# An eighth Strassen pair, a modulation row formed early and in place, and a down product that begins with two blocks kept in SBUF

## The chip, the cores and the metric

The kernel runs on one core of one Trainium2 chip. The time is device microseconds (us) of one execution of the whole layer, batch 1, 512 tokens, width 1024. It is given as the median of several runs; one more execution was recorded instruction by instruction, and every row below comes from that one.

## The reference

The layer is a hybrid mixer (an mLSTM and an S5 state space model, gated and mixed) followed by a convolutional gated FFN, each behind an adaptive layer norm. The change lies in the FFN and in what feeds it. Cut to that:

```python
def _conv_glu_ffn(h, w_ffn_up, w_ffn_conv, b_ffn_conv, w_ffn_down):
    val, gate = jnp.split(h @ w_ffn_up, 2, axis=-1)          # 1024 -> 2 x 2816
    gate = jax.nn.gelu(_causal_dwconv(gate, w_ffn_conv, b_ffn_conv))   # 3 taps along the tokens
    return (gate * val) @ w_ffn_down                          # 2816 -> 1024

mod = silu(c) @ w_ada + b_ada
sh1, sc1, g1, sh2, sc2, g2 = jnp.split(mod, 6, axis=-1)
...
h = _standardize(x) * (1.0 + sc2) + sh2
f = _conv_glu_ffn(h, w_ffn_up, w_ffn_conv, b_ffn_conv, w_ffn_down)
x = _layer_norm(ALPHA * x + (1.0 + g2) * f, ln2_gain, ln2_bias)
```

`g2` is one row of 1024 numbers, a product of the conditioning vector with 1024 x 1024 weights. The kernel multiplies it into the rows of `w_ffn_down` instead of into `f`.

## The kernel before

Products are in fp32 precision built from pairs: each operand is split into a high and a low part (a cast on ScalarE, line 226 or 1227, then a subtraction on VectorE, line 215), and one product of 128 x 128 weights with 128 x 512 activations is three matmuls (lines 247 to 249).

The FFN has 22 hidden blocks of 128 (`NF`), each with a gate product and a value product over 8 chunks of the width: 24 matmuls of 512 columns each. From block 0 on, the loop over `j` forms the blocks. A block whose number is in `FAST` is done together with its follower by `fast_and_plain`: block `j` by Strassen's scheme (its gate and value rows and the two token halves are the 2 x 2 matrix; seven products of 12 matmuls with 256 columns, line 1264), block `j + 1` in the plain way. Such a pair is called pair 6, pair 8 and so on after its first block; each Strassen product needs a combination of weights (`fast_operands`, VectorE line 212, tiles `hx`) split into halves (`half`, tiles `hb`), and combinations of activations that `x_combos` forms once, ahead of block `XJ` = 3.

PSUM tiles: the gate product of block `j` lies in `gtile[j % 2]` (two tiles called `acc`), the value product in `vtile[j % 2]` (two called `s`), and four tiles called `hd` serve the first two Strassen products, the gelu's scratch and whatever else asks. `gate_half` reads a gate tile by ScalarE once (line 1204) and by VectorE twice (line 207, 128x510 and 128x511, the two convolution taps), then forms the gelu (a Square and a Tanh on ScalarE, lines 567 and 569, each followed by one VectorE line 207). `val_half` multiplies by the value and either writes the block to DRAM (`spill`, blocks below `NSP` = 20) or keeps it split in SBUF (tiles `gab`).

`ada2_step` adds one eighth of `g2`'s product into two `s5h` tiles (`acc2[3]`): two loads from `wa` and two VectorE instructions (line 207). `MODS` lists after which blocks a step is done. At block `G2J` = 20, `grow` sums those tiles over the partitions with four matmuls against ones (line 951; they need the tiles split first, VectorE line 215) and forms the row in two `hh` tiles. At block `FJ` = 21, the first block of down weights is multiplied by `g2` and split (`scaled`: VectorE line 212, ScalarE and VectorE for the split).

Then `tail_product` runs the down product over the 22 blocks in the order of the list `down`: 14 places are streamed, each 24 matmuls onto eight PSUM tiles; the last eight are resident and go token block by token block, with the final layer norm behind each. `act_at` reads the spilled blocks back two places ahead. Tiles have tags with a fixed number of buffers (`BUFS`): `w`=2, `wh`=3, `wl`=3 for weights, `hb`=6, `hh`=7, `hx`=17, `s5h`=8.

Each engine takes its instructions in the fixed order that a scheduler wrote into the program when it was built, and all DMAs of the kernel are issued by one queue (SP) in its order. The scheduler follows the order of the code only loosely: it may place an instruction earlier or later on an engine, by its own estimate of when things are ready.

Of the kernel before, what the change touches and what calls it, by code (L numbers as in the profile page):

```python
# [16 lines left out]
P = 128  # L17
# [15 lines left out]
NF = 22  # L33
# [103 lines left out]
M2 = 2  # L137
MKR = 6
PF = 1
G2J = 20  # L140
FAST = (6, 8, 10, 12, 14, 16, 18)
XJ = 3
MODS = (5, 6, 8, 10, 12, 14, 16, 18)
NSP = 20
FJ = 21
QUICK = (1, 3)
LAST = ((0, 0, 512), (1, 0, 256), (1, 256, 512))
# [15 lines left out]
def _build(ctx, tc, nc, h):  # L163
# [14 lines left out]
    def bank(tag):  # L178
        return tl(tag, [P, 512], pool=ps)
# [10 lines left out]
    def hh(n=512, dt=F32, parts=P):  # L190
        return hx(n, dt, parts, "hh")
# [4 lines left out]
    def dma(o, i):  # L196
        return nc.sync.dma_start(o, i)  # L197

    def ts(o, i, a, b=None, op0=ALU.mult, op1=None):
        if op1 is None:  # L200
            V.tensor_scalar(o, i, a, None, op0=op0)
        else:
            V.tensor_scalar(o, i, a, b, op0=op0, op1=op1)

    def stt(o, i0, s, i1, op0=ALU.mult, op1=ALU.add, acc=None):
        if acc is None:
            V.scalar_tensor_tensor(o, i0, s, i1, op0=op0, op1=op1)  # L207
        else:
            V.scalar_tensor_tensor(o, i0, s, i1, op0=op0, op1=op1, accum_out=acc)
# [31 lines left out]
    def pair_of(x, tag):  # L241
        p = new_pair(tag)
        split_into(p[0], p[1], x)
        return p
# [698 lines left out]
        dma(r, h["rows"][i:i + 1, :].to_broadcast([P, D]))  # L943
        return [r[:, :512], r[:, 512:]]

    def grow(i, factor, tag="s5"):
        g = row(i)
        for n in range(2):
            o = bank(tag)
            for e, x in enumerate(pair_of(acc2[2 + i][n], "hh")):  # L950
                T.matmul(o, lhsT=onesr, rhs=x, start=e == 0, stop=e == 1)
            stt(g[n], o, 1.0, g[n], ALU.add, ALU.add)
            ts(g[n], g[n], factor)
        return g

# [256 lines left out]
    def val_half(j, gg, ov):  # L1212
        if len(ov) == 1:
            tt(gg, ov[0], gg)
        else:
            for i in range(2):
                sl = slice(256 * i, 256 * i + 256)
                tt(gg[:, sl], ov[i][:, 0:256], gg[:, sl])
        if j < NSP:
            dma(spill[j * P:(j + 1) * P, :], gg)  # L1220
            gp_.append(None)
        else:
            gp_.append(pair_of(gg, "gab"))

    def half(src):
        o = big((P, 2, 512), F32R, next(optag))
# [96 lines left out]
    first = []  # L1323
    for j in range(NF):
        if j == G2J:
            g2 = grow(1, 0.5, "hd")
        if j >= FJ:
            first.append(scaled(h["wfd"][len(first)], g2, None))
        if j == XJ:
            x_combos()  # L1330
        if j in FAST:
            fast_and_plain(j)
        elif j - 1 not in FAST:
            ou = {}
            for u in (2 * j + 1, 2 * j):
                if u in pre:
                    ou[u] = pre[u]
                else:
                    w = wsplit(h["wup"][u])
                    ou[u] = (gtile if u % 2 else vtile)[j % 2]  # L1340
                    up_mm(ou[u], w, slice(0, 512))
                if u % 2:
                    gg = gate_half(j, (ou[u],))
            val_half(j, gg, (ou[2 * j],))
        ada2_step(MODS.count(j))
    l2 = []

    def finish2(t, bk):
# [5 lines left out]
        for n in range(2):  # L1354
            dma(h["out"][t * P:(t + 1) * P, n * 512:(n + 1) * 512], r[n])
        yield
    down = list(range(NF))
    got = {}

    def act_at(k):  # L1360
        for kk in range(k, min(k + 3, NF)):
            j = down[kk]
            if kk in got:
                continue
            if j >= NSP:
                got[kk] = gp_[j]
                continue
            x = hh()
            dma(x, spill[j * P:(j + 1) * P, :])
            got[kk] = pair_of(x, "hx" if j % 7 < 3 else "s5h")  # L1370
        return got[k]

    tail_product(act_at, [h["wfd"][j] for j in down], g2, "hh", NF, 8, [("s5b", "s5b")] * 2 + [("hp", "hp")] * 4 + [("hb", "hb")] * 2, finish2, FDB, first)
# [17 lines left out]
```

## Time and profile before

| | |
|---|---|
| Median of 3 runs | 862.05 us (861.99 to 862.38) |
| The profiled execution | 859.15 us, of it 857.4 us from first to last instruction |
| TensorE (PE) busy | 818.5 us, 95% |
| VectorE (DVE) busy | 651.4 us, 76% |
| ScalarE (ACT) busy | 382.5 us, 45% |
| Mean granted TensorE clock | 0.997 of full speed |

The profiled execution lies 2.90 us below the median of the runs. In the profile, 527.23 us is the first matmul of block 4, 549.49 us the first of pair 6, 697.43 us the first of block 20, and 726.30 us the first of the down product. A row of a timeline gives start and duration in microseconds, engine, line, operation, the tile written and the tiles read (buffer numbers left out), the shape, and in square brackets the idle time of the engine before it with what ended that idle time.

### The profile page before, as it was taken

The page shows a single profiled execution, that of the slowest core. Times are in us where ns is not written, and L with a number is a line of the kernel's source. Part 1 is how long each engine was busy: PE and PEld are TensorE (multiplying, and loading weights), DVE is VectorE, ACT ScalarE, POOL GpSimd, SP SyncE. Part 2 cuts the span into 40 slices and gives each one's busy share as a digit, 9 for nine tenths or more (in the row PEclk, how much of TensorE's full clock was granted, in tenths as well). Part 3 has the DMA queues.
Part 4 walks back from the last instruction along what each step waited for, and adds up shares of the span by engine and source line. Part 5 has one row for each costly group of instructions (what it writes and reads, how often), then busy time and mean ns, then how long its engine had stood idle before and what let it go on. Part 6 is the DMA issues. An engine that isn't in the chain of part 4 may idle for free.

```text
span 857.4 us, 12051 instructions
## 1 busy us (share of the span) xinstructions
PE 818.5 (95%) x4358; PEld 672.8 (78%) x4358; DVE 651.4 (76%) x1260; ACT 382.5 (45%) x638; POOL 95.5 (11%) x233
## 2 busy tenths in 40 slices
PE   3999999999999999999999999999999997999996
PEld 1777868788687788888887988899888885888885
DVE  6557978789689774568978899878887667899144
ACT  4454564555546433232334565355555434545000
POOL 2871221122112100000002100000000000000000
PEclk9999999999999999999999999999999999999998
DMA  9922132222212233568655026544442233777011
GB/s 340 323 96 88 57 98 62 62 73 71 75 55 86 87 123 123 196 230 284 212 180 174 2 91 238 187 148 148 148 149 99 99 98 117 240 218 234 27 50 49
DMA packets 51179, 116.48 MB, mean 136 GB/s; under 512 B 14000, under 2 KB 14896, under 8 KB 51120
## 3 DMA queue, kind: packets, MB, share of 16 engines
q1 hardware_dynamic: 51120, 115.71, 40.9%
q8 instruction: 34, 0.56, 0.3%
q14 instruction: 25, 0.20, 0.1%
HBM read 106.25 MB, written 7.34 MB: 132 GB/s over the span
## 4 chain that ended last, share of the span: by engine, by line
PE 74%; DVE 13%; DMA 4%; ACT 4%; issue 2%; SPq 2%; POOL 0%; DVEq 0%; ACTq 0%; POOLq 0%
PE acc L247 10%; PE acc L249 10%; PE acc L248 10%; PE hd L247 6%; PE hd L248 6%; PE hd L249 6%; PE s L247 4%; PE s L249 4%; PE s L248 4%; PE acc L1264 3%; PE hd L1264 3%; DVE hh L207 3%; SPq L197 2%; DVE s5h L212 1%; DVE wl L215 1%
## 5 line engine op out<-in xcount | busy, mean ns | idle before, releaser
L226 ACT CAST wh<-w 128x1024 fp32r<-128x1024 f32 (+2 forms) x89 | 88.7, 999 | 126.8 <-PE acc L248 89.1
L215 DVE TENSOR_TENSOR wl<-w,wh 128x1024 fp32r<-128x1024 f32 (+2 forms) x89 | 103.4, 1165 | 34.5 <-ACT wh L226 33.7
L247 PE MATMUL acc<-hp,wh 128*128 128x512 f32 x256 | 103.0, 403 | 0.4 <-ACT hx L790 0.4
L249 PE MATMUL acc<-hp,wl 128*128 128x512 f32 x256 | 101.9, 398 | 0.0
L248 PE MATMUL acc<-hp,wh 128*128 128x512 f32 x256 | 101.7, 397 | 0.0
L1029 POOL TENSOR_SCALAR mov<-mov 128x1 f32<-128x1 f32 x6 | 3.6, 607 | 503.0 <-ACT acc L1028 330.8
L247 PEld LDWEIGHTS acc<-hp,wh 128*128 128x128 f32 x256 | 48.0, 188 | 14.2 <-issue 3.3
L249 PEld LDWEIGHTS acc<-hp,wl 128*128 128x128 f32 x256 | 48.1, 188 | 11.1 <-issue 0.4
L248 PEld LDWEIGHTS acc<-hp,wh 128*128 128x128 f32 x256 | 48.1, 188 | 10.7 <-issue 0.4
L207 DVE SCALAR_TENSOR_TENSOR s5h<-hh,k,s5h 128x512 f32<-128x512 f32 x56 | 39.7, 746 | 8.3 <-DMA hh<-in_wa 8.2
L207 DVE SCALAR_TENSOR_TENSOR hh<-hd,hh 128x512 f32<-128x512 f32 (+3 forms) x40 | 24.2, 607 | 15.7 <-POOL hh L859 8.4
L247 PE MATMUL hd<-s5b,wh 128*128 128x512 f32 (+1 forms) x88 | 31.9, 368 | 0.7 <-ACT s5b L1180 0.5
L248 PE MATMUL hd<-s5b,wh 128*128 128x512 f32 (+1 forms) x88 | 32.1, 366 | 0.2 <-DVE s5b L215 0.2
L249 PE MATMUL hd<-s5b,wl 128*128 128x512 f32 (+1 forms) x88 | 32.1, 366 | 0.0
L248 PE MATMUL acc<-hx,wh 128*128 128x512 f32 x77 | 30.4, 395 | 0.0
L247 PE MATMUL acc<-hx,wh 128*128 128x512 f32 x77 | 30.3, 394 | 0.0
L249 PE MATMUL acc<-hx,wl 128*128 128x512 f32 x77 | 30.3, 393 | 0.0
L1227 ACT CAST hb<-hx 128x512 fp32r<-128x512 f32 x28 | 17.4, 621 | 26.0 <-PE acc L1264 15.4
L226 ACT CAST hb<-hh 128x512 fp32r<-128x512 f32 (+3 forms) x37 | 20.3, 550 | 17.2 <-DVE hh L207 11.1
L212 DVE TENSOR_TENSOR hh<-w,hh 128x512 f32<-128x512 f32 x42 | 27.3, 684 | 0.5 <-DMA w<-in_wfd 0.3
L215 DVE TENSOR_TENSOR hb<-hh,hb 128x512 fp32r<-128x512 f32 (+3 forms) x37 | 22.1, 599 | 1.6 <-ACT hb L226 1.3
L1264 PEld LDWEIGHTS acc<-hp,hb 128*128 128x128 f32 x168 | 22.0, 188 | 1.3
(596 smaller groups left out, 2276.1 us busy)
## 6 DMA issues: line engine op xcount, KB each, us to landing
hh<-in_wa SPq DMA_DIRECT2D x64, 256.0 KB, 4.4
w<-in_win SPq DMA_DIRECT2D x30, 512.0 KB, 3.3
w<-in_wup SPq DMA_DIRECT2D x30, 512.0 KB, 3.4
w<-in_wfd SPq DMA_DIRECT2D x22, 512.0 KB, 4.1
hb<-in_wa SPq DMA_DIRECT2D x16, 512.0 KB, 7.3
gab<-in_wup SPq DMA_DIRECT2D x14, 512.0 KB, 4.0
spill<-hh SPq DMA_DIRECT2D x20, 256.0 KB, 2.3
hh<-spill SPq DMA_DIRECT2D x20, 256.0 KB, 3.4
```

The source lines that it names most:

```text
L197: return nc.sync.dma_start(o, i)
L207: V.scalar_tensor_tensor(o, i0, s, i1, op0=op0, op1=op1)
L212: V.tensor_tensor(o, a, b, op=op)
L215: V.tensor_tensor(o, a, b, op=ALU.subtract)
L226: A.copy(hi, x)
L247: T.matmul(o, lhsT=wh, rhs=xh, start=first, stop=False)
L248: T.matmul(o, lhsT=wh, rhs=xl, start=False, stop=False)
L249: T.matmul(o, lhsT=wl, rhs=xh, start=False, stop=last)
L1029: GP.tensor_scalar(v[:, 2:3], v[:, 0:1], v[:, 1:2], EPS * D, op0=ALU.add, op1=ALU.add)
L1227: A.copy(o[:, 0], src)
L1264: T.matmul(o[:, 0:256], lhsT=w[:, p, sl], rhs=x[k][y], start=first and k + i == 0, stop=k == 3 and i == 2, skip_group_check=True)
```

## The change

Pair 4 (blocks 4 and 5) is also done by Strassen's scheme. The eight steps of `g2` move forward (two after block 6, two after block 10, the last after block 14 instead of 18), and `g2` is formed ahead of pair 16 instead of block 20, in the two `s5h` tiles that held its sum, which it then occupies to the end; the bias row comes in through two passing `hh` tiles. Blocks 18 and 19 are not written to DRAM but kept split in two `hb` tiles, and the down product takes them first; the two last places, 20 and 21, stay as they were. The weights scaled at block 21 are then those of block 18. Spilled blocks are read back into `hx` and `s5h` tiles in turns of three and three instead of three and four.

```diff
-G2J = 20
-FAST = (6, 8, 10, 12, 14, 16, 18)
+G2J = 16
+FAST = (4, 6, 8, 10, 12, 14, 16, 18)
 XJ = 3
-MODS = (5, 6, 8, 10, 12, 14, 16, 18)
-NSP = 20
+MODS = (4, 6, 6, 8, 10, 10, 12, 14)
+NSP = 18
 FJ = 21
...
+    def grow_in_place(i, factor, tag):
+        g = acc2[2 + i]
+        for n in range(2):
+            r = hh()
+            dma(r, h["rows"][i:i + 1, n * 512:(n + 1) * 512].to_broadcast([P, 512]))
+            o = bank(tag)
+            for e, x in enumerate(pair_of(g[n], "hh")):
+                T.matmul(o, lhsT=onesr, rhs=x, start=e == 0, stop=e == 1)
+            stt(g[n], o, 1.0, r, ALU.add, ALU.add)
             ts(g[n], g[n], factor)
         return g
...
-            gp_.append(pair_of(gg, "gab"))
+            gp_.append(pair_of(gg, "hb" if j < 20 else "gab"))
...
-            g2 = grow(1, 0.5, "hd")
+            g2 = grow_in_place(1, 0.5, "hd")
         if j >= FJ:
-            first.append(scaled(h["wfd"][len(first)], g2, None))
+            first.append(scaled(h["wfd"][18 + len(first)], g2, None))
...
-    down = list(range(NF))
+    down = [18, 19] + list(range(NSP)) + [20, 21]
...
-            got[kk] = pair_of(x, "hx" if j % 7 < 3 else "s5h")
+            got[kk] = pair_of(x, "hx" if j % 6 < 3 else "s5h")
```

How the instructions stand afterwards, at three places. Line numbers in the changed kernel are 12 higher behind `grow` (1264 becomes 1276, 951 becomes 963).

**The start of pair 4.** TensorE before: the value product of block 3 (onto `s_1059`) ends, and the plain gate product of block 4 follows onto the gate tile `acc_4895`, last used by block 2.

```order
L248 MATMUL s_1059_4898<-hx_4732,wh_5357 128x512
L249 MATMUL s_1059_4898<-hx_4731,wl_5358 128x512
L247 MATMUL acc_4895<-s5b_4721,wh_5389 128x512
L248 MATMUL acc_4895<-s5b_4721,wh_5389 128x512
L249 MATMUL acc_4895<-s5b_4721,wl_5390 128x512
```

And now: two matmuls of block 5's plain gate product come first, onto `acc_4896`, the gate tile of block 3; then the first two Strassen products of block 4.

```order
L248 MATMUL s_1059_4898<-hx_4732,wh_5357 128x512
L249 MATMUL s_1059_4898<-hx_4731,wl_5358 128x512
L247 MATMUL acc_4896<-s5b_4721,wh_5436 128x512
L248 MATMUL acc_4896<-s5b_4721,wh_5436 128x512
L1276 MATMUL hd_5399<-s5b_4721,hb_5402 128x256 x3
L1276 MATMUL hd_5399<-s5b_4722,hb_5402 128x256 x3
L1276 MATMUL hd_5399<-s5b_4723,hb_5402 128x256 x3
L1276 MATMUL hd_5399<-s5b_4724,hb_5402 128x256 x3
L1276 MATMUL hd_5400<-hp_5271,hb_5418 128x256 x6
```

What moved: the tile that TensorE writes first behind block 3 is no longer the one freed by block 2 but the one that still holds block 3's gate. VectorE reads that gate in the two rows with `acc_4896`. Up to the row with `acc_4895` and 128x511 the queue of VectorE is the same in both kernels; before, these rows stood behind it:

```order
L212 TENSOR_TENSOR hx_5545<-hx_5544,gab_5539 128x512
L215 TENSOR_TENSOR wl_5390<-w_5387,wh_5389 128x1024
L207 SCALAR_TENSOR_TENSOR hd_5230<-hd_5230,hh_5225 128x512
L215 TENSOR_TENSOR wl_5430<-w_5427,wh_5429 128x1024
L207 SCALAR_TENSOR_TENSOR hh_5229<-hd_5230,hh_5225 128x512
L212 TENSOR_TENSOR hx_5546<-gab_5539,hx_5544 128x512
L212 TENSOR_TENSOR hh_5229<-s_1058_4897,hh_5229 128x512
L207 SCALAR_TENSOR_TENSOR hh_5345<-acc_4896,k_63,hh_5345 128x510
```

Now it is these, with the weight halves (`hb`) of pair 4 among them:

```order
L212 TENSOR_TENSOR hx_5393<-hx_5392,gab_5387 128x512
L212 TENSOR_TENSOR hx_5394<-gab_5387,hx_5392 128x512
L215 TENSOR_TENSOR hb_5402<-gab_5387,hb_5402 128x512
L207 SCALAR_TENSOR_TENSOR hd_5230<-hd_5230,hh_5225 128x512
L215 TENSOR_TENSOR hb_5418<-hx_5391,hb_5418 128x512
L215 TENSOR_TENSOR wl_5437<-w_5434,wh_5436 128x1024
L207 SCALAR_TENSOR_TENSOR hh_5229<-hd_5230,hh_5225 128x512
L215 TENSOR_TENSOR hb_5452<-hx_5392,hb_5452 128x512
L212 TENSOR_TENSOR hh_5229<-s_1058_4897,hh_5229 128x512
L207 SCALAR_TENSOR_TENSOR hh_5345<-acc_4896,k_63,hh_5345 128x510
L215 TENSOR_TENSOR hb_5468<-gab_5387,hb_5468 128x512
L207 SCALAR_TENSOR_TENSOR hh_5345<-acc_4896,k_63,hh_5345 128x511
```

Four weight halves and one more `hx` combination have come in ahead of the second reading of `acc_4896`, and one weight split of 1024 columns (`wl_5430`) has gone.

**The start of pair 16.** TensorE before: behind pair 14's last product, four matmuls of the plain gate product, then the Strassen products at once.

```order
L249 MATMUL s_1059_4898<-hx_4731,wl_6563 128x512
L247 MATMUL acc_4896<-s5b_4721,wh_6678 128x512
L248 MATMUL acc_4896<-s5b_4721,wh_6678 128x512
L249 MATMUL acc_4896<-s5b_4721,wl_6679 128x512
L247 MATMUL acc_4896<-s5b_4722,wh_6678 128x512
L1264 MATMUL hd_6641<-s5b_4721,hb_6644 128x256 x3
```

Now the whole plain gate product of block 17 (24 matmuls with `wh_6780`) and 16 matmuls of its value product (`wh_6882`) stand ahead of the four matmuls against ones (line 963, `k_183`), and the seven Strassen products follow in a row:

```order
L247 MATMUL s_1059_4898<-s5h_4727,wh_6882 128x512
L963 MATMUL hd_6711<-hh_6712,k_183 128x512
L248 MATMUL s_1059_4898<-s5h_4728,wh_6882 128x512
L249 MATMUL s_1059_4898<-s5h_4727,wl_6883 128x512
L963 MATMUL hd_6711<-hh_6713,k_183 128x512
L963 MATMUL hd_6722<-hh_6723,k_183 128x512
L1276 MATMUL hd_6743<-s5b_4721,hb_6746 128x256 x3
L963 MATMUL hd_6722<-hh_6724,k_183 128x512
```

The four matmuls have moved here from block 20's value product, and the plain products of pair 16 have moved ahead of its Strassen products.

**Blocks 20 and 21 and the start of the down product.** ScalarE before: the split of the first scaled down weights (`wh_7163` from `w_7161`, which is `w` times `g2`) stands ahead of the split of block 21's gate weights (`wh_7173`); the split of its value weights is `wh_7213`, and `hx_7255` is block 0 read back from DRAM.

```order
L1204 ACTIVATE hh_7117<-acc_4895,k_63 128x512
L226 CAST wh_7163<-w_7161 128x512
L226 CAST wh_7173<-w_7171 128x1024
L567 ACTIVATE hd_7122<-hh_7117 128x512
L226 CAST wh_7163<-w_7161 128x512
L569 ACTIVATE hd_7122<-hd_7122 128x512
L226 CAST gab_7158<-hh_7121 128x512
L226 CAST wh_7213<-w_7211 128x1024
```

Now (`wh_7235` the scaled weights, of block 18; `hb_7140` and `hb_7156` the kept blocks 18 and 19; `wh_7245` and `wh_7285` the weights of block 21):

```order
L226 CAST wh_7235<-w_7233 128x512
L567 ACTIVATE hd_7133<-hh_7125 128x512
L226 CAST wh_7235<-w_7233 128x512
L569 ACTIVATE hd_7133<-hd_7133 128x512
L226 CAST hb_7140<-hh_7132 128x512
L226 CAST hb_7156<-hh_7086 128x512
L226 CAST wh_7245<-w_7243 128x1024
L1216 ACTIVATE hh_7189<-acc_4895,k_63 128x512
L567 ACTIVATE hd_7194<-hh_7189 128x512
L569 ACTIVATE hd_7194<-hd_7194 128x512
L226 CAST wh_7285<-w_7283 128x1024
```

The scaled weights, and both kept blocks, are split ahead of block 20's gate (the row 1216 that reads `acc_4895`), where before they stood behind it. On TensorE the down product began with `acc_7245<-wh_7163,hx_7255`; it now begins with:

```order
L249 MATMUL s_1059_4898<-hx_4731,wl_7286 128x512
L247 MATMUL acc_7317<-wh_7235,hb_7140 128x512
L248 MATMUL acc_7317<-wl_7236,hb_7140 128x512
L249 MATMUL acc_7317<-wh_7235,hb_7140 128x512
L247 MATMUL acc_7318<-wh_7235,hb_7140 128x512
```

Its first operand is a block that VectorE finished before block 20, where before it was one that came back from DRAM.

## Rows read from the trace of the kernel before

**Rows 1.** The head of the profile's page: the span, and of each engine the busy time, its share of the span and the number of instructions.

```profile
span 857.4 us, 12051 instructions
...
PE 818.5 (95%) x4358; PEld 672.8 (78%) x4358; DVE 651.4 (76%) x1260; ACT 382.5 (45%) x638; POOL 95.5 (11%) x233
```

**Rows 2.** Busy time in three stretches of the FFN, columns: stretch, its length and TensorE's busy time (instructions), weight loads, VectorE, ScalarE, POOL, granted TensorE clock, DMA share, GB/s.

```profile
500.00:520.00 20.00, 18.96 (x95) 15.44 (x94) 19.29 (x32) 12.84 (x20) 0.00 (x0) 1.00 0.60 206
600.00:620.00 20.00, 20.00 (x125) 17.86 (x124) 16.64 (x27) 10.44 (x18) 0.00 (x0) 1.00 0.46 149
740.00:760.00 20.00, 20.00 (x88) 16.14 (x87) 17.26 (x28) 8.53 (x16) 0.00 (x0) 1.00 0.66 218
```

**Rows 3.** Timeline of TensorE: the first matmul of block 4, the first Strassen product of pair 6, and the first matmul of block 20.

```profile
527.23 0.39 PE L247 MATMUL acc<-s5b,wh 128*128 128x512 f32 x1
...
549.49 1.56 PE L1264 MATMUL hd<-s5b,hb 128*128 128x256 f32 x12
...
697.43 0.39 PE L247 MATMUL acc<-s5b,wh 128*128 128x512 f32 x1
```

**Rows 4.** Timeline of VectorE from 516 us on, while TensorE is in block 3.

```profile
516.07 1.22 DVE L215 TENSOR_TENSOR wl<-w,wh 128x1024 fp32r<-128x1024 f32 x1
517.21 0.68 DVE L207 SCALAR_TENSOR_TENSOR hh<-hd,hh 128x512 f32<-128x512 f32 x1
517.81 0.68 DVE L212 TENSOR_TENSOR hx<-gab,gab 128x512 f32<-128x512 f32 x1
518.41 0.68 DVE L212 TENSOR_TENSOR hh<-hd,hh 128x512 f32<-128x512 f32 x1
519.01 0.74 DVE L207 SCALAR_TENSOR_TENSOR hh<-acc,k,hh 128x510 f32<-128x510 f32 x1
519.66 0.68 DVE L212 TENSOR_TENSOR hx<-gab,hx 128x512 f32<-128x512 f32 x1
520.26 0.74 DVE L207 SCALAR_TENSOR_TENSOR hh<-acc,k,hh 128x511 f32<-128x511 f32 x1
520.92 0.68 DVE L212 TENSOR_TENSOR hx<-hx,gab 128x512 f32<-128x512 f32 x1
...
522.97 0.69 DVE L207 SCALAR_TENSOR_TENSOR hd<-hd,hh 128x512 f32<-128x512 f32 x1
```

**Rows 5.** Timeline of ScalarE in the same stretch.

```profile
520.75 1.05 ACT L226 CAST wh<-w 128x1024 fp32r<-128x1024 f32 x1 [1.60 <-DMA w<-in_wup]
521.70 0.61 ACT L1227 CAST hb<-hx 128x512 fp32r<-128x512 f32 x1
522.22 0.59 ACT L567 ACTIVATE hd<-hh 128x512 f32<-128x512 f32 x1
...
525.23 0.78 ACT L1204 ACTIVATE hh<-acc,k 128x512 f32<-128x512 f32 x1
```

**Rows 6.** Timeline of TensorE at the start of block 2, whose gate product (onto acc) and value product (onto s) are interleaved.

```profile
504.28 0.50 PE L247 MATMUL acc<-s5b,wh 128*128 128x512 f32 x1 [0.82 <-ACT wh L226]
...
505.23 0.50 PE L247 MATMUL s<-s5b,wh 128*128 128x512 f32 x1 [0.22 <-ACT wh L226]
```

**Rows 7.** Timeline of TensorE: the first matmul behind pair 14.

```profile
655.16 0.39 PE L247 MATMUL acc<-s5b,wh 128*128 128x512 f32 x1
```

**Rows 8.** Timeline of VectorE at the same place: the last instruction of pair 14, and the step of g2 that follows it.

```profile
660.76 0.42 DVE L212 TENSOR_TENSOR hh<-hh,hh 128x256 f32<-128x256 f32 x1
662.16 0.75 DVE L207 SCALAR_TENSOR_TENSOR s5h<-hh,k,s5h 128x512 f32<-128x512 f32 x1 [0.98 <-DMA hh<-in_wa]
```

**Rows 9.** Timeline of the DMA queue: issue of that step's two loads.

```profile
657.92 0.86 SPq L197 DMA_DIRECT2D hh<-in_wa  x2
```

**Rows 10.** Timeline of TensorE through blocks 20 and 21: the first of four matmuls against ones, the five waits, and the first matmul of the down product, which the last of them precedes.

```profile
703.70 0.40 PE L951 MATMUL hd<-hh,k 128*128 128x512 f32 x1
...
710.49 0.50 PE L247 MATMUL acc<-s5b,wh 128*128 128x512 f32 x1 [0.80 <-ACT wh L226]
...
711.89 0.50 PE L249 MATMUL acc<-s5b,wl 128*128 128x512 f32 x1 [0.67 <-DVE wl L215]
...
717.71 0.50 PE L247 MATMUL s<-s5b,wh 128*128 128x512 f32 x1 [0.47 <-ACT wh L226]
...
718.97 0.50 PE L249 MATMUL s<-s5b,wl 128*128 128x512 f32 x1 [0.54 <-DVE wl L215]
...
726.30 0.50 PE L247 MATMUL acc<-wh,hx 128*128 128x512 f32 x1 [1.95 <-ACT hx L226]
```

**Rows 11.** Timeline of ScalarE at the same place: the two casts wh_7163 and wh_7173 in one row, and the cast of block 0 read back.

```profile
708.87 1.57 ACT L226 CAST wh<-w 128x512 fp32r<-128x512 f32 x2 [3.98 <-DVE w L212]
...
725.63 0.61 ACT L226 CAST hx<-hh 128x512 fp32r<-128x512 f32 x1
```

**Rows 12.** Timeline of the DMA queue: issue of the load of block 21's value weights.

```profile
711.86 0.33 SPq L197 DMA_DIRECT2D w<-in_wup  x1
```

**Rows 13.** Timeline of VectorE: the value product of block 21 taken up, and its first idle times in the down product.

```profile
724.39 0.69 DVE L212 TENSOR_TENSOR hh<-s,hh 128x512 f32<-128x512 f32 x1 [1.26 <-PE s L249]
...
741.38 1.29 DVE L212 TENSOR_TENSOR hh<-w,hh 128x512 f32<-128x512 f32 x2 [0.32 <-DMA w<-in_wfd]
743.39 0.69 DVE L215 TENSOR_TENSOR hx<-hh,hx 128x512 fp32r<-128x512 f32 x1 [0.71 <-ACT hx L226]
```

**Rows 14.** Timeline of ScalarE: the last block read back and split for the resident stage.

```profile
798.93 0.62 ACT L226 CAST s5h<-hh 128x512 fp32r<-128x512 f32 x1 [4.82 <-PE hd L248]
```

More of the change, by code (lines that the diff above doesn't have):

```diff
@@ L944, in row_w, with grow @@
         return [r[:, :512], r[:, 512:]]
-    def grow(i, factor, tag="s5"):
+    def grow(i, factor):
         g = row(i)
         for n in range(2):
-            o = bank(tag)
+            o = bank("s5")
             for e, x in enumerate(pair_of(acc2[2 + i][n], "hh")):
@@ L952, in grow @@
             stt(g[n], o, 1.0, g[n], ALU.add, ALU.add)
+            ts(g[n], g[n], factor)
+        return g
+    def grow_in_place(i, factor, tag):
[7 more added lines that the diff above has]
+            stt(g[n], o, 1.0, r, ALU.add, ALU.add)
             ts(g[n], g[n], factor)
```

## The prediction

> **What bounds the kernel now.** I read the page's head first, then the windows, then the waits and timelines of the places that the change touches. TensorE is busy for 818.5 of 857.4 us [rows 1], so a change counts only if it takes work from TensorE or a wait from in front of it. Through most of the FFN it has no idle time at all: 20.00 of 20 us at 600 and at 740, while VectorE has 16.64 and 17.26 [rows 2]. At 500 to 520 it is otherwise: VectorE is busy for 19.29 of 20 us, it is working off the activation combinations and the gates of the first blocks, and there the order of its queue decides. The second place is the passage into the down product, 697.43 to 726.30, where TensorE waits five times [rows 10].
>
> **The eighth pair.** Blocks 4 and 5 in the plain way take 549.49 - 527.23 = 22.26 us for 96 matmuls of 512 columns, 0.232 each; the seven pairs from there to block 20 take 697.43 - 549.49 = 147.94, 21.13 each [rows 3]. A pair more saves 1.13 us of TensorE. It costs VectorE about 5 us: two splits of 1.14 us fewer, but seven halves and four combinations at 0.60 (distances of the starts [rows 4]; a half is the same operation and shape as a combination) and small change. In the steady state, at 600 us, VectorE has room for it [rows 2].
>
> **The wait it brings.** At the start of pair 4 that room is not there. TensorE is through with block 3 at 527.23 [rows 3]. Its next matmul then writes block 3's own gate tile (`acc_4896`), so it waits for VectorE's second tap on that tile; before, it wrote the tile of block 2, whose second tap began at 520.26 [rows 4]. When is the tap done? The queue of VectorE is unchanged to the combination at 520.92. From there, with 0.60 for each instruction of 512 columns: the fourth combination 521.52, a half 522.12, the gelu's first step 522.9 (it needs the Square that ends at 522.81 [rows 5]), a half 523.5, the split 524.1, gelu 525.24, half 525.84, the value of block 2 526.44, first tap 527.04, half 527.69, second tap 528.29, which lasts 0.74: 529.03. The first tap needs ScalarE's reading of the gate, which ended at 526.0 [rows 5] and is now some 0.5 later, still in time. So TensorE stands for about 1.85 us, all ready Strassen products behind it. What queues up on VectorE behind the tap (halves three to seven, the split of block 5's value weights) is needed 5 us later or more and isn't late. The pair's gain is thereby more than lost: -1.13 + 1.85 = +0.7.
>
> How sure is the 1.85? From below it is 0, if VectorE gains 1.8 us somewhere in 13 us; from above, each of the 19 instructions since 516.07 would take its duration (0.68) and not the distance of starts (0.60): 1.6 more, 3.4. The trace shows the distances in this very stretch [rows 4], so I take 1.85, with 1.5 to 2.2 as likely. The Trainium skill ("VectorE: DVE Perf Modes", section "The DRAIN you can't avoid") says that the next operation does not start until the pipeline has emptied; by that the wait would be the 3.4. The trace does not agree: starts lie 0.60 apart where the instructions last 0.68 [rows 4].
>
> **g2 ahead of pair 16.** The four matmuls against ones (0.93 us) move, they neither come nor go [rows 10]. They now stand 40 plain matmuls behind pair 14, that is 40 x 0.232 = 9.28 us after its end (655.16 [rows 7], so 664.44 on the axis of before). What they need: the step's loads are issued as early as in the trace [rows 9], and VectorE took the step up at 662.16 [rows 8]. Now a weight split stands ahead of it, which waits for a weight buffer that TensorE frees 24 matmuls in, at 660.73; cast 1.05 [rows 5] and split 1.14 end about 663.0; then two steps of 0.65, and casts and halves at 0.6. The first high half is there at about 664.4, the last low half at 665.6, and TensorE arrives at 664.44 and about 665.5. I charge 0.2 us, with 0 to 0.6. The row's further work (two additions, two scalings, under 2.5 us of VectorE) is needed only for the weights at block 20. The doubled steps behind blocks 6 and 10 add 2 x 0.65 us to pairs in which VectorE has over 3 us to spare; if that cover were gone, it would cost the 1.3 us. The two loads and two stores fewer for the spill cost and bring nothing: no wait of TensorE in the steady state ends on one.
>
> **Into the down product.** From block 20's first matmul to the down product's first it is 726.30 - 697.43 = 28.87 us. The 96 matmuls take 22.26, the four against ones 0.93; 5.68 is waiting and restarting. The five waits are 0.80, 0.67, 0.47, 0.54 and 1.95, together 4.43 [rows 10]. Their causes, and what becomes of them:
> - 0.80 and 0.67: ScalarE stood for 3.98 us on the weights times `g2`, and the split of block 21's gate weights stood behind that in its queue [rows 11]. `g2` is now there at about 669, some 40 us earlier.
> - 0.47 and 0.54: block 21's value weights were loaded only at 711.86 [rows 12], since the buffer was held by the same scaled weights. These are now split when pair 18's last weights are used up, at the start of block 20; the load starts some 11 us earlier, and 1 was lacking.
> - 1.95: the down product's first operand was block 0 read back, cast at 725.63 behind block 21's own chain [rows 11]. Now it is block 18, split before block 20. TensorE also needs eight PSUM tiles: the last to come free holds block 21's value, read by VectorE in 0.69 us [rows 13], and is reached 9 matmuls (2.1 us) into the product. Behind that, VectorE has two multiplications and two splits for the second place, under 4 us with what is between, inside the 5.57 us of the first place.
>
> I take the whole 5.68 as gained. Later the rate is TensorE's own: VectorE already had idle time at 741 and 743 [rows 13], and now has two blocks fewer to split. One wait moves: with three pairs of `s5h` tiles instead of four, block 17 gets its tiles only when the streaming ends. The trace shows the same wait, four places earlier [rows 14]. A cast of 0.62 and a split of 0.6 follow, and TensorE wants the block 15 matmuls (3.5 us) into the resident stage; 2 us are left, so 0.
>
> **Sum.** -1.13 + 1.85 + 0.2 - 5.68 = -4.76 us. The profiled execution would go from 859.15 to 854.4; the runs' median stands 2.90 higher, so 862.05 - 4.76 = 857.3 us, 0.55% faster.
>
> **Rivals.**
> - **No wait at pair 4** (14%): VectorE is through by 527, or TensorE finds other work. Everything else as above: 855.4. Against the first stand the distances in the queue [rows 4], against the second the order on TensorE [rows 6]: the value product's first matmul waited 0.22 us for its weights while the gate product's next chunk, with weights there since 504.28, stood behind it. The Trainium skill says the same ("TensorE: Matmul & The Clock Gate", "What happens when you issue a matmul": only weight loads are pulled ahead, matmuls stay in program order); by it the ready Strassen products can't fill the 1.85 us, and the sum stays 857.3.
> - **VectorE's instructions don't overlap** (4%): the wait is 3.4 us, 858.9. The rule on the DRAIN would have it so; the trace speaks against it [rows 4].
> - **A new wait at the down product's start** (9%): a PSUM tile, the second place's weights or the first blocks read back come late by as much as the old last wait, restart included, 2.1 us: 859.4. For it: at 724 VectorE was busy without a break till 741 [rows 13]. Against it: what it must have ready is less.
> - **The row g2 is late at pair 16** (6%): the step's loads land later behind a busier queue, or the buffer does; 1 to 2 us: 858.3 to 859.3.
> - **The wait of pair 4 repeats** (5%, slower): VectorE doesn't catch up, and each of the seven later pairs also finds the gate tile of the block before it unread. Price 1.85 each; from the fourth repeat on the kernel is slower than before by over 0.2%, with all seven 870.3. Against it: the later gate is read while 10 us of other products run, and VectorE has 3 to 4 us of idle time in each pair.
> - The rest (6%): two of the mishaps together, within 0.2% of before.
>
> **Chances and range.** The forecast has 56%, and 856.4 to 858.2 with its own bounds (wait 1.5 to 2.2, g2 0 to 0.6, the passage a few tenths either way). The range reaches to the case without the wait and to the one with a new wait: 855.0 to 859.8; outside are the last two. About 0.2% (1.7 us) is what a measurement can tell from no change: faster 89%, same 6%, slower 5%.
>
> **What the profile after would show.** Right: one wait of 1.5 to 2.2 us of TensorE in front of a gate product at about 527 us, ended by VectorE's 128x511 tap; eight pairs of 21.1 us; four matmuls against ones about 40 plain matmuls behind pair 14 with no wait over half a microsecond; no wait between block 20 and the middle of the down product. Wrong would be: no wait at 527, or the same one at later pairs; a wait of TensorE for `wl`, `wh`, `hx` or `s5h` after block 20; or one at the change from streamed to resident places, ended by a cast into `s5h`.

## The result

The changed kernel takes 857.25 us (median of 4 runs, 856.09 to 857.88) against 862.02 us of the kernel before in the same session: ratio 0.9945, 95% interval 0.9928 to 0.9962. Forecast were 857.3 us and 0.55% less, in the median; the profiled execution was forecast at 854.4.

The profiled execution took 856.97 us and its span is 855.3, only 2.1 shorter than before [rows 1]. Its clock axis is shifted: block 3 ends at 529.94 instead of 527.23, though every engine has the same instructions in the same order up to some 18 us before that. A stretch around 163 us with a granted clock of 0.57, which the execution of before did not have, makes 1.7 of these 2.71 us. The rest comes from the start of the execution: near 20 us matmuls of 512 columns start 0.23 us apart in the execution of before and 0.43 apart in this one, which puts it 1.7 us behind; 0.7 of that comes back ahead of block 3. So times are taken from here on from the end of block 3: from the moment at which the next matmul was due (the last one's start plus 0.23) to the start of the kernel's last matmul. That is 321.88 us before and 316.96 after, 4.92 less.

### The profile page after: what moved, and what is told of

It is laid out like the page before. It is cut to its first block, busy times and chain, and to the rows that moved or that the text cites. A ratio compares the mean times of both kernels' runs of the same rounds, so it can differ in the third digit from the quotient of the medians.

```text
span 855.3 us, 12133 instructions
## 1 busy us (share of the span) xinstructions
PE 820.1 (96%) x4394; PEld 676.6 (79%) x4394; DVE 655.7 (77%) x1272; ACT 386.4 (45%) x647; POOL 96.0 (11%) x233
## 4 chain that ended last, share of the span: by engine, by line
PE 73%; DVE 15%; ACT 4%; DMA 3%; issue 2%; SPq 2%; POOL 1%; DVEq 0%; ACTq 0%; POOLq 0%
PE acc L247 9%; PE acc L248 9%; PE acc L249 9%; PE hd L247 6%; PE hd L248 6%; PE hd L249 6%; PE acc L1276 4%; PE hd L1276 4%; PE s L247 3%; PE s L249 3%; PE s L248 3%; DVE hh L207 3%; SPq L197 2%; DVE s5h L212 1%; PE s L1276 1%
## 5 line engine op out<-in xcount | busy, mean ns | idle before, releaser
L226 ACT CAST wh<-w 128x1024 fp32r<-128x1024 f32 (+2 forms) x87 | 86.6, 998 | 116.4 <-PE acc L248 71.5
L215 DVE TENSOR_TENSOR wl<-w,wh 128x1024 fp32r<-128x1024 f32 (+2 forms) x87 | 101.1, 1163 | 24.3 <-ACT wh L226 23.5
L1239 ACT CAST hb<-hx 128x512 fp32r<-128x512 f32 x32 | 19.9, 622 | 25.3 <-PE acc L1276 14.4
L212 DVE TENSOR_TENSOR hh<-w,s5h 128x512 f32<-128x512 f32 x42 | 27.4, 685 | 0.4 <-DMA w<-in_wfd 0.4
L1276 PEld LDWEIGHTS acc<-hp,hb 128*128 128x128 f32 x192 | 24.9, 188 | 1.4 <-DVE s L212 0.4
```

Source lines behind the costliest of these rows:

```text
L212: V.tensor_tensor(o, a, b, op=op)
L215: V.tensor_tensor(o, a, b, op=ALU.subtract)
L226: A.copy(hi, x)
L1239: A.copy(o[:, 0], src)
L1276: T.matmul(o[:, 0:256], lhsT=w[:, p, sl], rhs=x[k][y], start=first and k + i == 0, stop=k == 3 and i == 2, skip_group_check=True)
```

## The profile after

The head of the page (span; busy time, share and instructions of each engine):

```profile
span 855.3 us, 12133 instructions
...
PE 820.1 (96%) x4394; PEld 676.6 (79%) x4394; DVE 655.7 (77%) x1272; ACT 386.4 (45%) x647; POOL 96.0 (11%) x233
```

Two windows of 2 us from the first half (columns as in [rows 2]; the granted clock is the third figure from the end):

```profile
162.00:164.00 2.00, 2.00 (x14) 2.00 (x12) 2.00 (x4) 0.33 (x1) 0.00 (x0) 0.57 0.03 8
164.00:166.00 2.00, 2.00 (x12) 2.00 (x12) 1.47 (x2) 0.00 (x0) 0.00 (x0) 0.58 0.29 84
```

TensorE at a clock of 0.57 and 0.58 for 4 us has done the work of 2.3: the 1.7 us above. What TensorE waited for from 500 us to the end (total, times, longest):

```profile
PE acc L247 <- DVE hh L207: 1.7, 1, 1.7
PE acc L247 <- ACT wh L226: 0.8, 1, 0.8
PE s L247 <- ACT wh L226: 0.2, 1, 0.2
```

The two lower lines are the start of block 2, as before [rows 6]. The five waits of [rows 10] are gone, one has come: 1.7 us, for line 207 of VectorE, the taps. TensorE at its place and at the places of the forecast (start, duration, line, tile, idle time before):

```profile
529.71 0.40 PE L249 MATMUL s<-hx,wl 128*128 128x512 f32 x1
531.84 0.47 PE L247 MATMUL acc<-s5b,wh 128*128 128x512 f32 x1 [1.73 <-DVE hh L207]
...
532.37 1.56 PE L1276 MATMUL hd<-s5b,hb 128*128 128x256 f32 x12
...
658.89 0.39 PE L247 MATMUL acc<-s5b,wh 128*128 128x512 f32 x1
...
668.17 0.45 PE L963 MATMUL hd<-hh,k 128*128 128x512 f32 x1
...
702.18 0.39 PE L247 MATMUL acc<-s5b,wh 128*128 128x512 f32 x1
...
724.45 0.40 PE L247 MATMUL acc<-wh,hb 128*128 128x512 f32 x1
...
846.90 0.28 PE L249 MATMUL hd<-hb,gab 128*128 128x256 f32 x1
```

Matmuls due at 529.94 start at 531.84: with the restart, 1.90 us are lost. At 668.17 the first matmul against ones follows its neighbour at the ordinary distance (667.94 + 0.23). Block 20 starts at 702.18 and the down product at 724.45, 22.27 us later, without a pause at either (the matmuls ahead of them start at 701.95 and 724.23). VectorE in front of the wait:

```profile
529.09 0.68 DVE L212 TENSOR_TENSOR hh<-s,hh 128x512 f32<-128x512 f32 x1
529.70 0.74 DVE L207 SCALAR_TENSOR_TENSOR hh<-acc,k,hh 128x510 f32<-128x510 f32 x1
530.35 0.68 DVE L215 TENSOR_TENSOR hb<-gab,hb 128x512 fp32r<-128x512 f32 x1
530.95 0.74 DVE L207 SCALAR_TENSOR_TENSOR hh<-acc,k,hh 128x511 f32<-128x511 f32 x1
```

The second tap ends at 531.69, and the waiting matmul starts 0.15 later. On the axis of before that end is 528.98; the forecast had 529.03. The same tap in the kernel before:

```profile
528.01 0.75 DVE L207 SCALAR_TENSOR_TENSOR hh<-acc,k,hh 128x511 f32<-128x511 f32 x1
```

It began 0.78 us behind the end of block 3 (527.23), and begins 1.01 behind it now (530.95 - 529.94). So the eighth pair has hardly made the tap later; what is new is that TensorE wants this tile at once. The section on the change counts four weight halves and one combination that have come in ahead of this tap. By the kernel before's own trace it is three halves and no combination, against one weight split that has gone: one half (at 527.41) and both combinations stood ahead of the tap there too.

All kernels by stretch, in microseconds from the traces: the wait at pair 4 with its restart, from there to block 20, blocks 20 and 21, the down product to its last matmul, and the sum. The rows from the third on are the experiments below, in their order. The kernel before has a median of 861.94 us in the session of the first four of them and 861.16 in that of the last four.

| kernel | median, ratio to before [95%] | wait | to block 20 | 20, 21 | down | sum |
|---|---|---|---|---|---|---|
| before | | 0 | 170.20 | 28.87 | 122.81 | 321.88 |
| changed | 857.25, 0.9945 [0.9928, 0.9962] | 1.90 | 170.34 | 22.27 | 122.45 | 316.96 |
| changed, again | 855.50, 0.9929 [0.9915, 0.9943] | 1.77 | 170.16 | 22.27 | 122.45 | 316.65 |
| changed, gate tiles exchanged | 853.06, 0.9896 [0.9880, 0.9912] | 0 | 170.26 | 22.27 | 122.45 | 314.98 |
| changed, without pair 4 | 854.24, 0.9902 [0.9885, 0.9919] | 0 | 171.23 | 22.27 | 122.73 | 316.23 |
| changed, tap made later | 862.84, 1.0008 [0.9993, 1.0023] | 7.36 | 172.56 | 22.27 | 122.45 | 324.64 |
| before + pair 4 | 861.51, 1.0004 [0.9988, 1.0021] | 1.65 | 169.13 | 27.85 | 124.06 | 322.69 |
| before + pair 4, tiles exchanged | 859.05, 0.9983 [0.9970, 0.9995] | 0 | 169.07 | 28.00 | 122.52 | 319.59 |
| before + `g2` moved | 857.99, 0.9966 [0.9952, 0.9979] | 0 | 171.25 | 24.99 | 122.71 | 318.95 |
| before + start of the down product | 858.17, 0.9957 [0.9941, 0.9972] | 0 | 170.20 | 148.82 together | | 319.02 |

Where the four matmuls against ones lie in the pairs (all with `g2` formed early), the column to block 20 holds their 0.93 us, elsewhere the next column does.

## Experiments

### The changed kernel again

> The changed kernel once more, to stand beside the next three on one chip: 857.2 us, 0.994 to 0.995 of before, by every theory. TensorE stands 1.9 us in front of pair 4 (last matmul of block 3 to first of the pair, less 0.23), and 317.0 us lie between the end of block 3 and the last matmul of the kernel. If the 1.9 us came from this one execution, it would be shorter than 1.5 or longer than 2.3 here.

The wait was there again, 1.77 us with its restart instead of 1.90; the sum 316.65 instead of 316.96. So two executions of one program differ by 0.3 us in this measure, and the wait belongs to the program. The median is another matter: 855.50 us and 0.9929, where 857.2 and 0.994 to 0.995 were expected. The ten runs of this kernel in the two sessions order themselves by the mean granted clock: 854.65 to 856.09 us at 0.998, 856.73 to 857.53 at 0.996, 857.88 at 0.994. The medians of the next two kernels, of the same session, lie 2.2 and 2.3 us below the expected ones as well, though their sums agree with it. So the sums are compared with what was expected, and medians only within a session.

### The two gate tiles of a pair exchanged

> The changed kernel, with the two gate tiles of a pair exchanged: block 5's plain gate product goes onto the tile of block 2, which VectorE has read some 6 us before, and block 4's later Strassen products onto the tile of block 3. Theory of the tile: the wait of 1.9 us in front of pair 4 is for that tile alone and goes away whole; nothing else is late, since the second tap ends some 1.9 us into the pair and the other tile is wanted 6 us into it: 315.1 us from the end of block 3 to the last matmul, median 855.3, 0.992 of before. Rival of the backlog: VectorE is behind as such, and the next thing that TensorE wants of it (the low half of block 5's weights, a weight half) is late by as much: 1 to 1.9 us of the wait come back within pair 4, median 856.3 to 857.2.

```diff
 def fast_and_plain(j):
     src = fast_operands(j)
-    b, d = gtile[j % 2], vtile[j % 2]
-    g2_, v2_ = gtile[1 - j % 2], vtile[1 - j % 2]
+    b, d = gtile[1 - j % 2], vtile[j % 2]
+    g2_, v2_ = gtile[j % 2], vtile[1 - j % 2]
```

TensorE from the end of block 3 on:

```profile
527.35 0.40 PE L247 MATMUL s<-hx,wh 128*128 128x512 f32 x1
528.05 0.39 PE L247 MATMUL acc<-s5b,wh 128*128 128x512 f32 x1
...
531.06 1.56 PE L1276 MATMUL hd<-s5b,hb 128*128 128x256 f32 x12
...
533.89 1.60 PE L1276 MATMUL acc<-hp,hb 128*128 128x256 f32 x12
```

VectorE's second tap on block 3's gate:

```profile
529.08 0.74 DVE L207 SCALAR_TENSOR_TENSOR hh<-acc,k,hh 128x511 f32<-128x511 f32 x1
```

The first plain matmul starts where it is due, three matmuls behind the row at 527.35. The tap comes no earlier than in the changed kernel: it starts 1.03 us after block 3's end (528.05), there 1.01 (529.94). VectorE is thus as far behind as it was, and nobody waits for it: TensorE writes the tile that the tap reads only at 533.89. 1.67 to 1.98 us shorter than the changed kernel's two traces, 314.98 where 315.1 was expected. The theory of the tile holds; the rival of the backlog, 1 to 1.9 us of the wait back within the pair, falls. At 0.9896 this version beats both kernels, and its interval does not touch that of the changed kernel in the same session.

### Without the eighth pair

> The changed kernel with blocks 4 and 5 plain again, all else kept. By the sum of the prediction pair 4 costs more than it gives (-1.13 and +1.9), so this is 0.8 us faster than the changed kernel: 316.2 us from the end of block 3 to the last matmul, median 856.5, 0.9935 of before, and no wait of TensorE in front of block 4. Rival: the eighth pair also relieves something later (VectorE has two weight splits fewer), and the kernel without it is slower than the changed one by up to 1.1 us, 858.3.

```diff
-FAST = (4, 6, 8, 10, 12, 14, 16, 18)
+FAST = (6, 8, 10, 12, 14, 16, 18)
```

316.23 us, where 316.2 was expected; TensorE's only waits behind 500 us are the two of block 2. So in the changed kernel pair 4 costs 0.42 or 0.73 us more than it gives, by the one or the other of that kernel's traces: 1.77 or 1.90 of wait, against 1.07 or 0.89 up to block 20 and 0.28 in the down product, of which more below. The medians (854.24 against 855.50) point the same way, but their intervals overlap. The size is uncertain, with one trace of this kernel and 0.3 us between two executions of the other.

### The tap made later

> The changed kernel with five multiplications by 1.0 of block 3's gate ahead of its two taps, each dependent on the one before. In the order as built VectorE has, ahead of the second tap, these five (0.35 each by the distance of a like row in the trace), and between them two weight halves, two combinations (0.60 each) and a weight split (1.14) that stood behind it: 5.3 us more. On TensorE the matmul that waits for the tap still stands first, and two Strassen products whose weights are ready stand behind it. Theory of a fixed order: the wait grows by the whole 5.3, to about 7.2 us, and since the work moved ahead of the tap is then done already, nothing else changes: 322.3 us from the end of block 3, median 862.5, about that of before. Rival, TensorE fills the wait with the ready products (2.9 us), or slack later in the pair takes it up: the wait grows by 2.4 or less, median 859.7 or less.

```diff
         A.activation(a, g, AF.Identity, bias=col("fb", j), scale=col("fw", 44 + j))
+        for _ in range(5 if j == 3 else 0):
+            ts(a, a, 1.0)
         for q in range(2):
```

VectorE: the first and the last of the five multiplications (line 201), what came between, and the second tap. Then TensorE, and windows of it with the granted clock as third figure from the end:

```profile
528.13 0.42 DVE L201 TENSOR_SCALAR hh<-hh 128x512 f32<-128x512 f32 x1
528.46 0.68 DVE L215 TENSOR_TENSOR hb<-gab,hb 128x512 fp32r<-128x512 f32 x1
...
531.27 1.22 DVE L215 TENSOR_TENSOR wl<-w,wh 128x1024 fp32r<-128x1024 f32 x1
532.41 0.42 DVE L201 TENSOR_SCALAR hh<-hh 128x512 f32<-128x512 f32 x1
...
534.60 0.74 DVE L207 SCALAR_TENSOR_TENSOR hh<-acc,k,hh 128x511 f32<-128x511 f32 x1
```

```profile
527.91 0.40 PE L249 MATMUL s<-hx,wl 128*128 128x512 f32 x1
535.50 0.77 PE L247 MATMUL acc<-s5b,wh 128*128 128x512 f32 x1 [7.19 <-DVE hh L207]
536.06 2.76 PE L1278 MATMUL hd<-s5b,hb 128*128 128x256 f32 x12
538.62 2.55 PE L1278 MATMUL hd<-hp,hb 128*128 128x256 f32 x12
541.00 0.40 PE L248 MATMUL acc<-s5b,wh 128*128 128x512 f32 x1
```

```profile
535.50:537.00 1.50, 1.50 (x6) 1.40 (x7) 1.50 (x3) 0.48 (x1) 0.00 (x0) 0.50 0.38 156
537.00:539.00 2.00, 2.00 (x11) 2.00 (x11) 2.00 (x4) 0.72 (x2) 0.00 (x0) 0.50 0.00 0
539.00:541.00 2.00, 2.00 (x12) 2.00 (x11) 2.00 (x4) 0.75 (x2) 0.00 (x0) 0.56 0.74 260
541.00:543.00 2.00, 2.00 (x11) 1.64 (x10) 1.15 (x3) 0.89 (x2) 0.00 (x0) 1.00 0.35 133
```

The idle time is 7.19 us, 7.36 with the restart, where 7.2 was expected. The two Strassen products behind it (their weight halves were split before 526.3) did not move into it: they follow at 536.06 and 538.62. So TensorE does not fill such a wait, and the rival falls. The sum is 324.64, though, where 322.3 was expected. The missing 2.4 us stand in the rows behind the wait: the two products of 12 matmuls take 2.76 and 2.55 us, in the changed kernel 1.56 and 1.60, at a granted clock of 0.50, which is the 1.2 GHz level. Behind the wait of 1.73 us in the changed kernel the same product takes 1.56, at full clock. A long wait cost a third more than itself. That the median, 862.84, is near the expected 862.5 is luck: these 2.4 us stand against the 2.2 by which the session's medians lie lower.

### Pair 4 alone

> The kernel before with pair 4 alone added (FAST takes in 4, nothing else). Theory of the sum: the pair gives 1.13 and the wait for block 3's gate tile takes 1.9 in front of it, the passage at blocks 20 and 21 keeps its five waits: from the end of block 3 to the last matmul 321.88 - 1.13 + 1.9 = 322.65 us, median 0.8 above before, 1.001. Rival: the two weight splits fewer on VectorE shorten the passage too, and the kernel is faster than before by up to 1 us.

```diff
-FAST = (6, 8, 10, 12, 14, 16, 18)
+FAST = (4, 6, 8, 10, 12, 14, 16, 18)
```

322.69 us where 322.65 was expected, which is luck: the parts are others. TensorE's waits:

```profile
531.07 0.47 PE L247 MATMUL acc<-s5b,wh 128*128 128x512 f32 x1 [1.48 <-DVE hh L207]
713.58 0.50 PE L247 MATMUL acc<-s5b,wh 128*128 128x512 f32 x1 [1.04 <-ACT wh L226]
714.98 0.50 PE L249 MATMUL acc<-s5b,wl 128*128 128x512 f32 x1 [0.66 <-DVE wl L215]
728.05 0.50 PE L247 MATMUL acc<-wh,hx 128*128 128x512 f32 x1 [1.96 <-ACT hx L226]
```

Two windows behind the last of them:

```profile
728.00:730.00 2.00, 1.95 (x6) 1.51 (x7) 2.00 (x5) 1.56 (x3) 0.00 (x0) 0.62 0.04 13
730.00:732.00 2.00, 2.00 (x6) 1.61 (x5) 2.00 (x5) 0.72 (x2) 0.00 (x0) 0.52 0.54 161
```

The wait at pair 4 is 0.25 shorter than taken. Blocks 20 and 21 have three waits in place of five, 1.02 us less: those for block 21's value weights are gone, whose load lands earlier after its issue. The DMA issues from 705 to 722 us, the line of this load (KB, median us from issue to landing), in the kernel before:

```profile
w<-in_wup SPq DMA_DIRECT2D x1, 512.0 KB, 4.7
```

and in this one:

```profile
w<-in_wup SPq DMA_DIRECT2D x1, 512.0 KB, 3.3
```

And the down product lost 1.3 us (124.06 against 122.81) or 1.7 (by the windows) to a granted clock of 0.62 and 0.52 behind the wait of 1.96; behind the same wait of 1.95 the execution of before stayed at 1.00. Without that stretch the sum would be 321.4 or less, half a microsecond below before. The rival, that the passage gets shorter too, is borne out, if not by its reason: it is the load that is faster. Why is open: the kernel of the next section has 3.4 us for it, the last one below, without pair 4, 4.6. The median, at 1.0004, tells no difference.

### Pair 4 with the tiles exchanged, on the kernel before

> The kernel before with pair 4 and with the two gate tiles of every pair exchanged. Theory of the tile: the pair now gives its 1.13 and nothing waits: 320.75 us from the end of block 3, median 1.1 below before, 0.9987; with the exchange all pairs run at 21.13 us. Rival: the exchange by itself also changes the later pairs or the start of block 20, which begins on the other tile: a difference of more than half a microsecond between the end of pair 4 and block 20.

(Both edits shown above.) No wait at pair 4, and 169.07 us for eight pairs: 21.13 each, to the hundredth what the seven took [rows 3]. The exchange changes nothing else between pair 4 and block 20. In block 20 one wait is new, in front of the first matmul against ones:

```profile
702.75 0.50 PE L951 MATMUL hd<-hh,k 128*128 128x512 f32 x1 [0.61 <-ACT hh L226]
```

The wait for block 21's gate weights is smaller there, 0.36 in place of 1.04, and the passage takes 28.00 us where pair 4 without the exchange has 27.85. The sum, 319.59, lies 1.16 below the expected 320.75: 0.87 of it is the passage with the faster load, 0.3 the down product.

### The row g2 alone

> The kernel before with the row g2 alone moved: the steps after blocks 5, 6, 6, 8, 10, 10, 12, 14, formed in place ahead of pair 16, three pairs of s5h tiles for the blocks read back; the down product keeps its order and begins with block 0. Theory of separate causes: the four waits of blocks 20 and 21 go (2.48 by the rows, 3.53 with the restarts behind them), the fifth, for block 0 read back, stays at 1.95: 318.4 us from the end of block 3 to the last matmul, median 3.5 below before, 0.996. Rival of the one chain: block 0 comes back at a time that hangs on the queue and on tiles that come free, not on block 21; then the fifth wait grows by what the others lost, up to 5.5, and the median stays within 1 us of before.

```diff
-G2J = 20
+G2J = 16
-MODS = (5, 6, 8, 10, 12, 14, 16, 18)
+MODS = (5, 6, 6, 8, 10, 10, 12, 14)
...
-            g2 = grow(1, 0.5, "hd")
+            g2 = grow_in_place(1, 0.5, "hd")
...
-            got[kk] = pair_of(x, "hx" if j % 7 < 3 else "s5h")
+            got[kk] = pair_of(x, "hx" if j % 6 < 3 else "s5h")
```

The wait that is left:

```profile
727.08 0.50 PE L247 MATMUL acc<-wh,hx 128*128 128x512 f32 x1 [2.56 <-ACT hx L226]
```

ScalarE in front of it:

```profile
725.29 0.62 ACT L226 CAST gab<-hh 128x512 fp32r<-128x512 f32 x1 [1.90 <-DVE hh L212]
725.88 0.62 ACT L226 CAST wh<-hh 128x512 fp32r<-128x512 f32 x1
726.41 0.62 ACT L226 CAST hx<-hh 128x512 fp32r<-128x512 f32 x1
```

The four waits of blocks 20 and 21 are gone and the fifth stays: separate causes. It has grown by 0.6, since a cast of the second place's weights now stands ahead of block 0's in ScalarE's queue; hence 318.95 and not 318.4. Block 0 came with block 21's chain and no later, so the rival of the one chain falls.

### The start of the down product alone

> The kernel before with the down product's start alone changed: blocks 18 and 19 kept in two hb tiles and taken first, the weights scaled at block 21 are those of block 18, g2 is still formed at block 20. Theory of separate causes: the fifth wait (1.95, 2.2 with its restart) goes, the other four stay in kind, since the scaled weights and block 21's weights still hang on g2 (one matmul with the scaled weights now stands ahead of block 21's gate product and waits for them): 319.7 us from the end of block 3, median 2.2 below before, 0.9975. Rival: the waits for scaled weights only shift, the second place's weights are late behind the first, and under 1 us is gained; or block 18's operand was the only cause, and more than 4 us is gained.

```diff
-NSP = 20
+NSP = 18
...
-            gp_.append(pair_of(gg, "gab"))
+            gp_.append(pair_of(gg, "hb" if j < 20 else "gab"))
...
-            first.append(scaled(h["wfd"][len(first)], g2, None))
+            first.append(scaled(h["wfd"][18 + len(first)], g2, None))
...
-    down = list(range(NF))
+    down = [18, 19] + list(range(NSP)) + [20, 21]
```

TensorE's waits in blocks 20 and 21:

```profile
709.32 0.47 PE L247 MATMUL acc<-wh,hb 128*128 128x512 f32 x1 [0.23 <-DVE hh L207]
710.17 0.50 PE L247 MATMUL acc<-s5b,wh 128*128 128x512 f32 x1 [0.38 <-ACT wh L226]
...
711.56 0.50 PE L249 MATMUL acc<-s5b,wl 128*128 128x512 f32 x1 [0.20 <-DVE wl L215]
...
717.32 0.50 PE L247 MATMUL s<-s5b,wh 128*128 128x512 f32 x1 [0.38 <-ACT wh L226]
...
718.58 0.50 PE L249 MATMUL s<-s5b,wl 128*128 128x512 f32 x1 [0.30 <-DVE wl L215]
```

The fifth wait is gone and the other four are there in kind, but smaller: 0.38, 0.20, 0.38 and 0.30 for 0.80, 0.67, 0.47 and 0.54. Matmuls of the down product have come in among them (the one at 709.32 is the first) and do useful work where TensorE stood. 319.02 us, 0.7 below the expected; the median's interval, 0.9941 to 0.9972, leaves the expected 0.9975 just outside. The two edits alone save 2.93 and 2.86 us and together, as the kernel without pair 4 has them, 5.65. Each had its own waits in the main, but that the gains add up so well is in part chance: the row `g2` alone lost 0.6 at the fifth wait, and this edit alone won some 1.0 (idle times of 1.49 for 2.48) at the waits that belong to `g2`.

## Why the prediction was right

- **The number:** the sum of the terms is borne out within half a microsecond (4.92 and 5.23 us less in the two executions, for 4.76). That the median met it to 0.05 us is luck, since the other session gave the same kernel 855.50 us, 6.4 below the kernel before. The profiled execution took 856.97 and not 854.4: it was 2.71 us late at the end of block 3, on which the sum had nothing.
- **The eighth pair, -1.13:** right. Eight pairs took 169.07 where nothing disturbed them.
- **The wait it brings, 1.85:** 1.90, 1.77 and 1.65 in three executions. Its cause (the tile of block 3's gate), what ends it (the 128x511 tap) and the order on TensorE held: with another tile the wait was 0, with a later tap 7.36, with ready products behind it. The tap's end fell within 0.05 us of the sum over VectorE's queue at 0.60 an instruction. With that the rivals without a wait and without overlap on VectorE fall: the rows at 529.09 to 530.95 start 0.60 to 0.65 apart and last 0.68 to 0.74. The sentence of the Trainium skill that the prediction weighed ("VectorE: DVE Perf Modes", "The DRAIN you can't avoid") would have given 3.4 and is not borne out here; the same paragraph goes on that an operation which is not held starts earlier, and with that these rows agree.
- **That the pair's gain is more than lost, +0.7:** the kernel without the pair was 0.42 to 0.73 us shorter. It holds only in the company of the other edits. Added alone to the kernel before, the pair also came with a shorter passage (1.02 and 0.87 us), which the sum did not contain; in the changed kernel nothing is left there to shorten.
- **g2 ahead of pair 16, 0.2:** 0.08 (the pair took 22.14 us, which is 21.13 and 0.93 and 0.08). The first matmul against ones came 9.28 us behind pair 14 (668.17 - 658.89), at the place that was worked out, and its operand was there.
- **The passage, -5.68:** 28.87 has become 22.27; with the 0.93 that moved away that is -5.67. Both halves of the reason were tried apart, and each was worth about half, with the crossing-over told above.
- **Afterwards, 0:** the down product took 122.45 instead of 122.81. 0.11 is the restart behind the old last wait, which lies in this stretch. The other 0.25 isn't explained; kernels with pair 4 have 122.4 to 122.5 and those without 122.6 to 122.7 when the restart is taken off and the one with the lower clock left out. It lies behind the streamed places: from the first resident matmul to the last it is 44.25 us in all five programs with pair 4, and 44.58 to 44.61 in the three without it that were read. The wait of the last block read back cost TensorE nothing, as foreseen, but its time was misread: ScalarE's cast stood for 4.98 us ([rows 14] had 4.82) and began at 797.04, one place of the down product before the streaming ended (802.65), not at its end. VectorE's last multiplication by `g2` is at 783.7, so the two `s5h` tiles of `g2` come free behind it and not at the very end; the next cast into such a tile, at 789.08, came while the other three pairs were still being read.

```profile
797.04 0.62 ACT L226 CAST s5h<-hh 128x512 fp32r<-128x512 f32 x1 [4.98 <-PE hd L248]
```

By stretches: +1.90, then 170.34 - 170.20 = +0.14 (where -1.13 + 0.93 + 0.2 = 0 was expected; 0.07 of it is the slower second matmul behind the wait, and 0.19 a pause in pair 12 that the second execution does not have), -6.60, -0.36, and +0.03 behind the last matmul: -4.89, where the sum was -4.76. No repeat of the wait at later pairs: their first matmuls follow without a pause.

## What to carry to other kernels

When a stage is rearranged, look at which PSUM tile its first matmul writes and who reads that tile last: here TensorE stood for it with ready work behind, 1.73 us and in one experiment 7.19, and exchanging two tiles, at no cost, was worth more (1.7 to 2.0 us) than the pair of Strassen products itself (1.13). Where an engine is behind, add up its queue at the distance of starts, not at durations; over 12 instructions that gave the wait within two tenths. And edits that shorten the same passage should be tried apart and together: added alone, the eighth pair came with 1.0 us less there, of which nothing was left beside the two others.

## What the runs showed that was not expected

A wait can cost more than itself. Behind 7.19 us without a matmul the granted clock was 0.50 (the 1.2 GHz level), and TensorE lost another 2.4 us before it was back at 1.00. The Trainium skill ("TensorE: Matmul & The Clock Gate", "HAM oscillation — how this bites in real kernels") warns that gaps in TensorE's work bring the lower clock back; this trace agrees, with those numbers. Behind waits of nearly 2 us it went either way: 1.00 behind 1.95 us in the kernel before, 0.62 and 0.52 behind 1.96 us with pair 4 alone, at a price of 1.3 to 1.7 us. It is so ahead of the FFN as well: near 160 us TensorE has a wait of 1.6 to 1.7 us in all ten traces, and behind it three of them show a granted clock of 0.50 to 0.69 and seven 1.00. What decides between the two is not shown by these runs.

The load of block 21's value weights, 512 KB, landed 3.3 or 3.4 us after its issue in two kernels (the kernel before with pair 4) and 4.6 or 4.7 us in two others (the kernel before, and that with the start of the down product alone); what makes the difference is open.
